# One FFN block instead of two taken plainly before the products by seven

## The chip, the cores and the metric

The kernel runs on one core of a Trainium2 chip. The metric is the device time of one execution in microseconds (us); shown is the median of three runs. A trace of one profiled execution gives start, duration and waits of each instruction on the engines: PE (TensorE, matmuls) with its weight loads (PEld), DVE (VectorE), ACT (ScalarE), POOL (GpSimd) and SP (SyncE, which issues DMAs).

## What is computed

The reference is one layer of a decoder for 1024 prompt positions and 64 sample positions, width 1024: a token mixer (a short convolution and two kinds of attention) with an output projection, then a dense SwiGLU FFN, each behind a modulated RMSNorm. The change touches the FFN alone, and of it the gate and up projections:

```python
def swiglu(h, w_gate_up, w_down):
    gate, up = jnp.split(h @ w_gate_up, 2, axis=-1)
    return (jax.nn.silu(gate) * up) @ w_down

    x = x + gate1 * (mix @ w_out)
    x = x + gate2 * swiglu(rmsnorm(x, g_ffn) * (1 + scale2) + shift2, w_gate_up, w_down)
```

The FFN's inner width is 2816, in the kernel 22 blocks of 128.

## The kernel before

Activations lie transposed: channels on the partitions (eight parts of 128), positions along the row. The 1088 positions are taken in three groups (GRP) of 366, 366 and 356; the third holds the 64 sample positions. Every product in float32 is made of three fast matmuls (mm3, L200, lines 206 to 208): weight and activation are each split into a high and a low part, and high by high, high by low and low by high are summed in PSUM. So each 128 x 512 piece of weights is loaded by SP (load, L97, tile wraw, five buffers), its high part copied by ACT (L92) and its low part subtracted by DVE (L93) into a tile wsp (four buffers). PSUM has three banks with the tag g (ps_g), two each with s and t, and one with o.

The FFN's part of the program runs as follows.

1. While the sample attention streams its caches, the output projection, the second norm and FFN blocks 0 to 3 are done for groups 0 and 1 alone.
2. In the pool "mid", the third group catches up: w_out (L928 ff.), sums of squares and root (second_rstd, rstd, L794), and the normalised, modulated and split activations h2[2] (second_norm, L820; lines 828 to 837 on DVE, ACT and POOL, part by part, in tiles tmp). Behind it in the program, NPRE blocks from block 20 on (FE = 20) make their gate and up products for groups 0 and 1 in the plain way (gate_up, L839), into rows u_ff.
3. In the pool "ffn", blocks 0 to 3 make gate and up for the third group. Between them sums_step (L964, lines 956 to 974) builds the sums of activations that the products by seven need, one of four steps behind each block: 12 DVE operations and 4 ACT copies (L961) a step, in four buffers tw. Then follows the down product of blocks 0 to 3 for the third group: eight output tiles of 12 matmuls, each added to the residual row by add_gated (L773, and for the sample columns L777, which writes ts, and L778).
4. The pairs (20, 21), (4, 5), ... (18, 19) follow. A block that was taken plainly needs the third group only, and a split of its u_ff (L861, L862). Every other block goes through gate_up_2x2 (L977): groups 0 and 1 are seen as a 2 x 2 block matrix with the input halves, and gate and up of both come out of seven products of 4 x 3 matmuls with 366 columns instead of eight; the third group is multiplied plainly beside them (4 x 12 matmuls). POOL makes four combinations of the weights for it (L981 to L984), DVE adds the products up (L1003 to L1023). After each pair its down product for all three groups follows.

The order of instructions on each engine is fixed when the program is built: it is written as above, and a scheduler moves instructions of independent work past each other by its own estimate of times. Each engine then goes through its list in order.

```python
        second_norm(2, second_rstd(2))
        first = [row("u_ff") for _ in range(NPRE)]
        for f, u in enumerate(first):
            gate_up(FE + f, u, None, (0, 1))
...
                if FE <= f < FE + NPRE:
                    u = first[f - FE]
                    split_hid(u, hh, 0, GRP[2][0])
                    gate_up(f, u, hh, (2,))
                else:
                    gate_up_2x2(f, hh)
```

Of the kernel before, what the change touches and what calls it, by code (L numbers as in the profile page):

```python
# [49 lines left out]
FPOOL = ((2, 3, 4), (1, 2, 3, 4, 5), (2, 4, 7))  # L50

MODN = (2, 1, 1, 0, 1, 0, 1, 1, 2, 1, 2, 0)
NPRE = 2

PACE = (1, 1, 1, 1, 0)

# [9 lines left out]
def _build(nc, tc, d, cst, rows, actp, stream, psum):  # L66
# [14 lines left out]
    def row(name):  # L81
        return rows.tile([128, T], F32, tag="row", bufs=ROWS, name=name)
# [734 lines left out]
    def second_rstd(g):  # L817
        return rstd(GRP[g], NADD, acc_tile(g))

    def second_norm(g, r):  # L820
        c0, n = GRP[g]
        m = min(n, SEQ - c0)
        h2[g] = act_tile()
        for k in range(KC):
            t = tmp()
            hi, lo = h2[g][:, 0, k, :n], h2[g][:, 1, k, :n]
            shift = MOD[:, 24 + k, 0:1]
            V.scalar_tensor_tensor(t[:, :m], x1[k][:, c0:c0 + m], MOD[:, 32 + k, 0:1], r[:, :m],
                                   op0=OP.mult, op1=OP.mult)
            S.activation(hi[:, :m], t[:, :m], AF.Identity, bias=shift)  # L830
            V.scalar_tensor_tensor(lo[:, :m], t[:, :m], shift, hi[:, :m].bitcast(F32), op0=OP.add, op1=OP.subtract)
            if g == 2:
                V.tensor_tensor(t[:, m:n], x1[k][:, c0 + m:c0 + n], r[:, m:n], op=OP.mult)
                V.tensor_tensor(bi(t[:, m:n]), bi(t[:, m:n]), modb(32 + k), op=OP.mult)
                V.tensor_tensor(bi(t[:, m:n]), bi(t[:, m:n]), modb(24 + k), op=OP.add)
                S.activation(hi[:, m:n], t[:, m:n], AF.Copy)
                G.tensor_tensor(lo[:, m:n], t[:, m:n], hi[:, m:n].bitcast(F32), op=OP.subtract)
# [87 lines left out]
    with tc.tile_pool(name="mid", bufs=1) as mid:  # L925
# [5 lines left out]
# [3 lines that stand above are left out]
# [3 lines left out]
    with tc.tile_pool(name="ffn", bufs=1, reuse_waits="tile") as ff:  # L937
# [4 lines left out]
        def hid_tile():  # L942
            return ff.tile([128, 2, T], F32R, tag="hid", bufs=2, name="hid")
# [104 lines left out]
        for f0, nf in FF_GROUPS[1:]:  # L1048
            hid = []
            for f in range(f0, f0 + nf):  # L1050
                hh = hid_tile()
                if FE <= f < FE + NPRE:
                    u = first[f - FE]
# [173 lines left out]
```

## Time and profile before

| | us |
|---|---|
| median of 3 runs | 1385.34 |
| lowest, highest | 1382.9, 1385.4 |
| the profiled execution | 1385.72 |
| its span in the trace | 1383.8 |
| mean granted TensorE clock | 0.989 of full speed |

The profiled execution's own time is its span and about 2 us around it. In the page, the first part gives the busy time of each engine; the chain follows the work that ended last back from the end. A row of a timeline is start, duration, engine, line, operation, and in brackets how long the engine had been idle before it and what it waited for. Matmuls overlap: each row shows some 0.33 us, but they start about 0.165 us apart.

### The profile page before, as it was taken

How to read it: one execution, taken by the hardware profiler on the slowest of the kernel's cores; microseconds unless marked ns; L12 is line 12 of the kernel's file. 1: busy time of each engine (PE TensorE's matmuls, PEld its weight loads, DVE VectorE, ACT ScalarE, POOL GpSimd, SP SyncE). 2: the span in 40 equal slices, each digit the busy share in tenths (PEclk: the TensorE clock that was granted, in tenths of full speed). 3: DMA queues.
4: the chain of work that ended last, by engine and by line, in shares of the span. 5: the costliest groups of instructions: out<-in, count | busy, mean ns of one | idle time of the engine just before them, and what ended most of it. 6: DMA issues, size and time to landing. Idle time of an engine off the chain costs nothing.

```text
span 1383.8 us, 23859 instructions
## 1 busy us (share of the span) xinstructions
PE 1340.4 (97%) x9097; PEld 1279.6 (92%) x9097; DVE 851.8 (62%) x2016; ACT 597.0 (43%) x1228; POOL 200.0 (14%) x283
## 2 busy tenths in 40 slices
PE   7999999999999998999999999999999999999994
PEld 5889999988898897889999999999999999999994
DVE  4557768356676336334679766666666666665657
ACT  5487875467765325223355323232323232323243
POOL 2042320201101000000010111111111111111114
PEclk9999999999999999999999999999999999999997
DMA  9342431354415778676544412141414242323103
GB/s 360 117 156 99 139 108 32 117 166 133 146 24 205 269 263 305 209 252 230 155 130 130 123 61 92 48 166 60 154 62 153 76 138 88 133 88 127 45 30 130
DMA packets 77190, 190.90 MB, mean 138 GB/s; under 512 B 14051, under 2 KB 23811, under 8 KB 76291
## 3 DMA queue, kind: packets, MB, share of 16 engines
q1 hardware_dynamic: 73376, 135.67, 29.9%
q10 hardware_dynamic: 3536, 53.65, 10.9%
q8 instruction: 72, 1.18, 0.3%
q14 instruction: 46, 0.35, 0.1%
q0 software_dynamic: 160, 0.04, 0.0%
HBM read 181.32 MB, written 59.33 MB: 174 GB/s over the span
## 4 chain that ended last, share of the span: by engine, by line
PE 87%; DVE 4%; DMA 4%; ACT 3%; issue 2%; POOL 1%; SPq 0%; POOLq 0%; ACTq 0%; DVEq 0%
PE ps_g L206 19%; PE ps_g L207 19%; PE ps_g L208 19%; PE ps_s L207 3%; PE ps_s L206 3%; PE ps_s L208 3%; PE ps_t L206 2%; PE ps_t L207 2%; PE ps_t L208 2%; PE ps_o L584 2%; PE ps_t L575 2%; PE ps_o L703 1%; PE ps_s L531 1%; DMA wraw<-in_w_in 1%; PE ps_s L669 1%
## 5 line engine op out<-in xcount | busy, mean ns | idle before, releaser
L206 PE MATMUL ps_g<-act,wsp 128*128 128x366 f32 (+1 forms) x1192 | 396.7, 334 | 4.3 <-DVE u_ff L846 2.0
L207 PE MATMUL ps_g<-act,wsp 128*128 128x366 f32 (+1 forms) x1192 | 395.3, 332 | 0.0
L208 PE MATMUL ps_g<-act,wsp 128*128 128x366 f32 (+1 forms) x1192 | 392.5, 331 | 0.0
L92 ACT ACTIVATE wsp<-wraw 128x512 fp32r<-128x512 f32 x232 | 145.7, 631 | 286.6 <-PE ps_g L208 185.3
L93 DVE TENSOR_TENSOR wsp<-wraw,wsp 128x512 fp32r<-128x512 f32 x232 | 166.3, 718 | 150.3 <-ACT wsp L92 144.6
L206 PEld LDWEIGHTS ps_g<-act,wsp 128*128 128x128 f32 x1192 | 225.2, 189 | 13.1 <-issue 4.1
L207 PEld LDWEIGHTS ps_g<-act,wsp 128*128 128x128 f32 x1192 | 225.6, 189 | 3.6 <-issue 2.5
L208 PEld LDWEIGHTS ps_g<-act,wsp 128*128 128x128 f32 x1192 | 225.1, 189 | 2.1 <-issue 1.2
L206 PE MATMUL ps_g<-hid,wsp 128*128 128x366 f32 (+3 forms) x464 | 152.6, 331 | 4.2 <-DVE ts L777 3.3
L207 PE MATMUL ps_g<-hid,wsp 128*128 128x366 f32 (+3 forms) x464 | 152.3, 328 | 1.8 <-DVE hid L862 1.7
L208 PE MATMUL ps_g<-hid,wsp 128*128 128x366 f32 (+3 forms) x464 | 152.6, 329 | 0.0
L206 PEld LDWEIGHTS ps_g<-hid,wsp 128*128 128x128 f32 x464 | 87.6, 189 | 6.9 <-issue 3.3
L92 ACT ACTIVATE wsp<-tw 128x512 fp32r<-128x512 f32 x64 | 40.5, 633 | 122.3 <-PE ps_g L208 58.9
L207 PEld LDWEIGHTS ps_g<-hid,wsp 128*128 128x128 f32 x464 | 87.9, 189 | 2.6 <-DVE hid L862 2.4
L207 PE MATMUL ps_s<-act,wsp 128*128 128x366 f32 x272 | 90.2, 332 | 0.0
L206 PE MATMUL ps_s<-act,wsp 128*128 128x366 f32 x272 | 90.1, 331 | 0.0
L208 PE MATMUL ps_s<-act,wsp 128*128 128x366 f32 x272 | 90.0, 331 | 0.0
L208 PEld LDWEIGHTS ps_g<-hid,wsp 128*128 128x128 f32 x464 | 87.8, 189 | 0.0
L773 DVE SCALAR_TENSOR_TENSOR p_q<-ps_g,MOD,p_q 128x366 f32<-128x366 f32 (+3 forms) x99 | 55.5, 571 | 50.4 <-PE ps_g L208 50.3
L773 DVE SCALAR_TENSOR_TENSOR p_qc<-ps_g,MOD,p_qc 128x366 f32<-128x366 f32 (+3 forms) x99 | 56.6, 572 | 35.0 <-PE ps_g L208 33.1
L981 POOL TENSOR_TENSOR tw<-wraw 128x512 f32<-128x512 f32 x16 | 21.9, 1367 | 346.4 <-DMA wraw<-in_w_gu 267.9
L545 ACT ACTIVATE Sb<-Sb,st 128x257 f32<-128x257 f32 (+5 forms) x96 | 60.6, 632 | 20.4 <-DVE st L537 19.7
(337 smaller groups left out, 2319.3 us busy)
## 6 DMA issues: line engine op xcount, KB each, us to landing
wraw<-in_w_gu SPq DMA_DIRECT2D x112, 256.0 KB, 2.8
wraw<-in_wmod SPq DMA_DIRECT2D x64, 256.0 KB, 3.7
raw<-in_bk SPq DMA_DIRECT2D x30, 512.0 KB, 6.2
raw<-in_bv SPq DMA_DIRECT2D x30, 512.0 KB, 7.4
wraw<-in_w_in SPq DMA_DIRECT2D x36, 256.0 KB, 4.2
wraw<-in_w_d SPq DMA_DIRECT2D x36, 256.0 KB, 2.6
mraw<-in_wmod SPq DMA_DIRECT2D x32, 256.0 KB, 5.5
wraw<-in_w_out SPq DMA_DIRECT2D x32, 256.0 KB, 3.2
```

What stands on the lines that cost most here:

```text
L92: S.activation(sp[:, 0, :], raw, AF.Copy)
L93: (V if not state["sub"] or state["n"] % state["sub"] else G).tensor_tensor(sp[:, 1, :], raw, sp[:, 0, :].bitcast(F32), op=OP.subtract)
L206: PE.matmul(ps[:, :n], lhsT=w_hi, rhs=a(0, ak), start=first and j == 0, stop=False, **kw)
L207: PE.matmul(ps[:, :n], lhsT=w_hi, rhs=a(1, ak), start=False, stop=False, **kw)
L208: PE.matmul(ps[:, :n], lhsT=w_lo, rhs=a(0, ak), start=False, stop=last and j == m - 1, **kw)
L531: PE.matmul(ps[:, :sn], lhsT=QH[:, qsl], rhs=KS[hd][:, kk], start=True, stop=False)
L545: S.activation(Sb[:, :ne], Sb[:, :ne], AF.Exp, scale=-1.0, bias=m, accum_out=st[:, 3:4])
L575: PE.transpose(pt[:, col:col + 128], Sb[:, (kb - k0) * 128:(kb - k0 + 1) * 128], ident)
L584: PE.matmul(po[:, q0:q0 + w], lhsT=Vt[:, kb, hd].rearrange("p a b -> p (a b)"), rhs=PT[:, hl, c0:c0 + w], start=fresh, stop=ch is chunks[- ...
L669: PE.matmul(ps[32 * j:32 * j + 32, :n], lhsT=Q[:, 2 * j + par, :], rhs=keys[par][:, j, :n], start=(par == 0), stop=(par == 1))
L773: ins = V.scalar_tensor_tensor(x1[m][:, c0:c0 + k], ps[:, :k], MOD[:, gate + m, 0:1], x1[m][:, c0:c0 + k], op0=OP.mult, op1=OP.add)
L981: G.tensor_tensor(t1, b12, b11, op=OP.subtract)
```

## The change

```diff
-NPRE = 2
+NPRE = 1
```

Block 21's gate and up products for groups 0 and 1 are no longer made in step 2, and its third group no longer by the plain form in step 4. Block 21 goes through gate_up_2x2 as blocks 4 to 19 do. Block 20 stays as it is.

On PE, the first place is the end of block 20's plain up product (ps_g with wsp_8106 before and wsp_8105 after; act_6253 and act_6278 are groups 0 and 1, act_7935 is the third group). Before:

```order
L208 MATMUL ps_g_8074<-act_6278,wsp_8106 128x366
L206 MATMUL ps_g_8135<-act_6253,wsp_8139 128x366
L207 MATMUL ps_g_8135<-act_6253,wsp_8139 128x366
L208 MATMUL ps_g_8135<-act_6253,wsp_8139 128x366
L206 MATMUL ps_g_8135<-act_6253,wsp_8139 128x366
```

Now:

```order
L208 MATMUL ps_g_8073<-act_6278,wsp_8105 128x366
L206 MATMUL ps_g_8148<-act_7935,wsp_8151 128x356
L207 MATMUL ps_g_8148<-act_7935,wsp_8151 128x356
L208 MATMUL ps_g_8148<-act_7935,wsp_8151 128x356
L206 MATMUL ps_g_8148<-act_7935,wsp_8151 128x356
```

The 96 matmuls of block 21 on groups 0 and 1 are gone from here; block 0's gate for the third group, which reads the newly normalised tile, comes directly behind block 20.

On DVE, the second place is behind the third group's normalisation, where the sums begin (tw, sa and act_6278 are written by sums_step, wsp are weight splits, u_ff_8009 is block 21's row, u_8147 block 0's row for the third group). Before:

```order
L967 TENSOR_TENSOR tw_8350<-tw_8348,tw_8350 128x366
L93 TENSOR_TENSOR wsp_8313<-wraw_8311,wsp_8313 128x512
L969 TENSOR_TENSOR tw_8348<-tw_8352,tw_8348 128x366
L962 TENSOR_TENSOR sa1_8268<-tw_8350,sa1_8268 128x366
L846 TENSOR_TENSOR u_ff_8009<-u_ff_8009,ps_g_8198 128x366
L971 TENSOR_TENSOR tw_8352<-tw_8350,tw_8352 128x366
L962 TENSOR_TENSOR act_6278<-tw_8348,act_6278 128x366
```

Now:

```order
L967 TENSOR_TENSOR tw_8224<-tw_8222,tw_8224 128x366
L969 TENSOR_TENSOR tw_8222<-tw_8226,tw_8222 128x366
L93 TENSOR_TENSOR wsp_8282<-wraw_8280,wsp_8282 128x512
L962 TENSOR_TENSOR sa1_8142<-tw_8224,sa1_8142 128x366
L971 TENSOR_TENSOR tw_8226<-tw_8224,tw_8226 128x366
L962 TENSOR_TENSOR act_6278<-tw_8222,act_6278 128x366
L846 TENSOR_TENSOR u_8147<-u_8147,ps_g_8184 128x356
L93 TENSOR_TENSOR wsp_8299<-wraw_8297,wsp_8299 128x512
```

The sums stand at the same place behind the normalisation; the splits between them now belong to blocks 0 and 1 of the third group, and block 21's multiplication is gone.

On DVE, the third place is in the third group's down product of blocks 0 to 3 (L773 and L777 read its output tiles: before 8697 is the third, 8719 the fourth; now 8571 the third, 8593 the fourth). Before:

```order
L773 SCALAR_TENSOR_TENSOR p_q0_2107<-ps_g_8697,MOD_106,p_q0_2107 128x292
L93 TENSOR_TENSOR wsp_8744<-wraw_8742,wsp_8744 128x512
L778 TENSOR_TENSOR cv_2828<-cv_2828,ts_8672 128x64
L93 TENSOR_TENSOR wsp_8766<-wraw_8764,wsp_8766 128x512
L778 TENSOR_TENSOR cv_4877<-cv_4877,ts_8694 128x64
L93 TENSOR_TENSOR wsp_8788<-wraw_8786,wsp_8788 128x512
L777 TENSOR_TENSOR ts_8716<-ps_g_8697,MOD_106 128x64
```

Now:

```order
L773 SCALAR_TENSOR_TENSOR p_q0_2107<-ps_g_8571,MOD_106,p_q0_2107 128x292
L93 TENSOR_TENSOR wsp_8618<-wraw_8616,wsp_8618 128x512
L969 TENSOR_TENSOR tw_8507<-tw_8511,tw_8507 128x366
L93 TENSOR_TENSOR wsp_8640<-wraw_8638,wsp_8640 128x512
L962 TENSOR_TENSOR sa1_8142<-tw_8509,sa1_8142 128x366
L778 TENSOR_TENSOR cv_2828<-cv_2828,ts_8546 128x64
L93 TENSOR_TENSOR wsp_8662<-wraw_8660,wsp_8662 128x512
L778 TENSOR_TENSOR cv_4877<-cv_4877,ts_8568 128x64
L971 TENSOR_TENSOR tw_8511<-tw_8509,tw_8511 128x366
L773 SCALAR_TENSOR_TENSOR p_q1_3224<-ps_g_8593,MOD_106,p_q1_3224 128x292
L962 TENSOR_TENSOR act_6278<-tw_8507,act_6278 128x366
L93 TENSOR_TENSOR wsp_8684<-wraw_8682,wsp_8684 128x512
```

The next row now is L777 of tile 8571. Before, all sums were done ahead of this place; now the last step's stand between the down product's evacuations, four of them ahead of the third tile's L777, and so does the fourth tile's L773.

## The prediction

> **What bounds the kernel now.** I read the page first: which engine is full, and what the chain that ended last is made of.
>
> ```profile
> PE 1340.4 (97%) x9097; PEld 1279.6 (92%) x9097; DVE 851.8 (62%) x2016; ACT 597.0 (43%) x1228; POOL 200.0 (14%) x283
> PE 87%; DVE 4%; DMA 4%; ACT 3%; issue 2%; POOL 1%; SPq 0%; POOLq 0%; ACTq 0%; DVEq 0%
> ```
>
> PE is busy for 97% of the span and holds 87% of the chain, so a matmul that goes away should be worth its own time, unless another engine comes to be late. DVE's 62% is an average; what counts is its share in the stage that the change shortens. That stage runs from the first plain gate and up product of block 20 to the end of block 21's third group. The second view is a table of busy times by stretch; the third is the chain of waits cut to 690 to 800 us.
>
> ```profile
> 691.70:725.30 33.60, 33.60 (x207) 33.60 (x206) 23.43 (x70) 17.71 (x36) 3.61 (x8) 1.00 0.41 133
> 725.30:757.00 31.70, 31.70 (x195) 31.70 (x194) 30.30 (x62) 18.20 (x37) 0.00 (x0) 1.00 0.43 126
> 757.00:772.70 15.70, 15.51 (x97) 15.25 (x96) 11.57 (x32) 6.08 (x10) 0.00 (x0) 1.00 0.45 135
> 772.70:788.40 15.70, 15.70 (x98) 15.70 (x97) 9.16 (x15) 6.92 (x13) 1.29 (x1) 1.00 0.43 132
> by line: PE ps_g L206 32.6%; PE ps_g L207 32.0%; PE ps_g L208 31.8%; PE ps_s L207 0.6%; PE ps_s L811 0.6%; PE ps_s L206 0.6%; PE ps_s L208 0.6%; PE ps_t L807 0.5%; DVE cv L773 0.5%; issue 0.1%; DVE ts L777 0.1%
> ```
>
> The columns after the stretch's length are busy us of PE, PEld, DVE, ACT and POOL. PE never stops before 757 us, but in 725.3 to 757 DVE is busy 30.30 of 31.70 us. There are two nearly full engines side by side. The change takes 16 us of PE work out from in front of that stretch, and hardly any DVE work.
>
> **The matmuls.** PE's rows give the stage borders (start us, duration); the last row is the page's group for POOL's weight combinations.
>
> ```profile
> 691.71 0.33 PE L206 MATMUL ps_g<-act,wsp 128*128 128x366 f32 x1
> 704.17 0.41 PE L207 MATMUL ps_g<-act,wsp 128*128 128x366 f32 x1
> 725.27 0.32 PE L206 MATMUL ps_g<-act,wsp 128*128 128x356 f32 x1
> 772.66 0.33 PE L206 MATMUL ps_g<-act,wsp 128*128 128x356 f32 x1
> 788.36 0.33 PE L206 MATMUL ps_g<-hid,wsp 128*128 128x366 f32 x1
> L981 POOL TENSOR_TENSOR tw<-wraw 128x512 f32<-128x512 f32 x16 | 21.9, 1367 | 346.4 <-DMA wraw<-in_w_gu 267.9
> ```
>
> Blocks 20 and 21, groups 0 and 1: 192 matmuls and the norm's few small ones, from 691.71 to 725.27. The last 125 of them start at 704.17 (counted in the order, behind the small ones at L811) and take 21.1 us, 0.169 each; block 21's 96 are 16.2 us, so block 20 ends near 709.0. The next 288 matmuls (192 of gate and up, 96 of the down product, all third group) take 47.4 us, 0.1645 each; 96 more, to 788.36, finish the two plain blocks.
>
> Block 21 was 96 + 48 = 144 matmuls. By seven products it is 7 x 12 = 84 plus the same 48: 132. Removed: 12 x 0.169 = **2.0 us** of PE. Splits stay at eight for the block and loads go from eight to four; POOL gets four operations of 1.37 us (the L981 row) and DVE seven operations where two multiplications stood before. These lie in the stretch after 757 us, where DVE is busy 9.16 to 11.57 of 15.70 us, so I cost them at nothing; without that cover POOL's four would cost 5.5 us.
>
> **The third group's normalisation.** In the order, PE's next work after block 20 now needs it; before, block 21 stood in between. DVE, ACT and POOL make it, part by part (eight parts of 128 channels); POOL's operation ends each.
>
> ```profile
> 704.46 0.52 DVE L828 SCALAR_TENSOR_TENSOR tmp<-cv,MOD,ps_s 128x292 f32<-128x292 f32 x1 [1.50 <-PE ps_s L811]
> 710.26 0.32 POOL L837 TENSOR_TENSOR act<-tmp,act 128x64 fp32r<-128x64 f32 x1 [1.21 <-ACT act L836]
> 713.83 1.03 POOL L837 TENSOR_TENSOR act<-tmp,act 128x64 fp32r<-128x64 f32 x2 [3.25 <-ACT act L836]
> 718.97 0.66 POOL L837 TENSOR_TENSOR act<-tmp,act 128x64 fp32r<-128x64 f32 x1 [0.34 <-ACT act L836]
> 704.40:719.40 15.00, 13.80 (x47) 1.00 0.43 141
> 719.40:759.30 39.90, 37.56 (x77) 1.00 0.41 119
> ```
>
> The last two rows are DVE alone: 13.80 of 15.00 us busy in the norm, so it will not come sooner. DVE's order there is the same as before but for one split. From 709.0 PE has parts 0 to 2: 18 matmuls, 3.0 us, to 712.0. Part 3 ends near 714.3: PE idles 2.3 us. After that parts arrive about as fast as PE uses them, with the next block's gate in between, and the last is there at 719.6. This wait alone costs **2.3 us**; the eight parts' covering work was block 21.
>
> **DVE after the normalisation.** This is the larger term. Behind the norm DVE's order has the sums for the products (48 operations), mixed with the splits that PE needs at once. The ends and the paces come from these rows:
>
> ```profile
> 716.75 0.94 DVE L831 SCALAR_TENSOR_TENSOR act<-tmp,MOD,act 128x292 fp32r<-128x292 f32 x2
> 718.78 0.69 DVE L93 TENSOR_TENSOR wsp<-wraw,wsp 128x512 fp32r<-128x512 f32 x1 [0.95 <-ACT wsp L92]
> 727.59 0.69 DVE L93 TENSOR_TENSOR wsp<-wraw,wsp 128x512 fp32r<-128x512 f32 x1
> 728.19 0.54 DVE L962 TENSOR_TENSOR sa<-tw,sa 128x366 fp32r<-128x366 f32 x1
> 728.64 0.54 DVE L967 TENSOR_TENSOR tw<-tw 128x366 f32<-128x366 f32 x1
> 762.10 0.52 DVE L773 SCALAR_TENSOR_TENSOR cv<-ps_g,MOD,cv 128x292 f32<-128x292 f32 x1 [2.82 <-PE ps_g L208]
> 762.54 0.22 DVE L777 TENSOR_TENSOR ts<-ps_g,MOD 128x64 f32<-128x64 f32 x1
> 762.67 0.52 DVE L773 SCALAR_TENSOR_TENSOR cv<-ps_g,MOD,cv 128x292 f32<-128x292 f32 x1
> 762.90 0.41 PE L206 MATMUL ps_g<-hid,wsp 128*128 128x356 f32 x1 [0.19 <-DVE ts L777]
> ```
>
> Start to start, a split takes 0.60 us, a sum 0.45, an evacuation 0.44, the short copy ts 0.13. The down product has three PSUM banks: its fourth tile waits for ts of the first (the 762.90 row), its sixth for ts of the third. In the new order 80 DVE operations run from the first sum up to that ts: 18 splits, 45 sums, 12 of 0.44 and 5 of 0.13, 10.8 + 20.3 + 5.3 + 0.7 = 37.0 us. The same sum over before's 76 operations up to 759.3 gives 36.8, and the window measured 37.56 busy; scaled, 37.7. The first sum can start when the norm's last operation is done, 717.7, and one split more stands ahead: 718.3. I add 0.6 of idle at the first split, whose buffer PE frees only with the norm's last part. So the sixth tile starts at 718.3 + 37.7 + 0.6 = 756.6, and three tiles of 12 matmuls, 5.9 us, end the stage at 762.5. From 709.0 that is 53.5 us where before needed 47.4: **+6.1 us**. The 2.3 us of the norm lies inside it, since DVE, not PE, sets the end. Bounds: with DVE's idle between 0 and the 2.3 us that it had before, and a start between 718.2 and 719.4, the end is 761.8 to 765.3, so +5.4 to +8.9; below, if DVE's work doesn't hold PE at all, only 2.3.
>
> **The new pair border.** Block 21 as products ends with a split that the down product waits for. Before, this pair had no such wait at 788.36; the later pairs show what it costs:
>
> ```profile
> 859.65 0.44 PE L207 MATMUL ps_g<-hid,wsp 128*128 128x366 f32 x1 [1.75 <-DVE hid L862]
> 929.86 0.44 PE L206 MATMUL ps_g<-hid,wsp 128*128 128x366 f32 x1 [0.15 <-DVE cv L773]
> 998.29 0.44 PE L206 MATMUL ps_g<-hid,wsp 128*128 128x366 f32 x1 [0.24 <-DVE cv L773]
> 857.48 1.72 POOL L983 TENSOR_TENSOR tw<-wraw 128x512 f32<-128x512 f32 x1
> 858.00 1.60 DVE L862 TENSOR_TENSOR hid<-u,hid 128x366 fp32r<-128x366 f32 x1
> ```
>
> I take **+0.2 us**, as most do. The bound above is about 2.0 (the 1.75 and 0.15 to 0.24 behind it): at 858.00 DVE's split took 1.60 us beside POOL, against 0.54 for the like operation at 728.19. If that collision moves away from the pair at 859, the change gains 2.0 instead.
>
> **The clock.** PE's rows after a wait of like size, and the granted clock (behind the count):
>
> ```profile
> 577.79 0.44 PE L206 MATMUL ps_g<-act,wsp 128*128 128x366 f32 x1 [2.00 <-DVE u_ff L846]
> 579.00:582.50 3.50, 3.50 (x14) 0.51 0.93 336
> 582.50:585.00 2.50, 2.50 (x18) 1.00 0.80 231
> 860.00:865.00 5.00, 4.76 (x26) 1.00 0.16 61
> ```
>
> After 2.00 us of idle the clock was 0.51 for 3.5 us, 1.7 us lost; after the 1.75 us at 859.65 it stayed at 1.00. My two waits (2.3 at the norm, about 2 at the down product's sixth tile) stand near the first. A fall at the norm is hidden, since DVE sets the end; one at the sixth tile is not. I take nothing, with 1.7 us as the other end. [...]
>
> **Sum.** -2.0 + 6.1 + 0.2 = **+4.3 us** on the profiled execution's 1385.72 us (span 1383.8): 1390.0. The median of the three runs is 0.4 lower; from it, 1389.6. PE is full to the last group, so nothing behind the stage takes this back.
>
> **Rivals.** (1) *Only the norm's wait costs*: DVE keeps ahead because PE, once late by 2.3 us, asks later. -2.0 + 2.3 + 0.2 = +0.5: 1385.8. For it: DVE is not late for any split in before. Against: PE would reach the sixth tile at 709.0 + 252 x 0.1645 + 2.3 = 752.8, 34.5 us after DVE's first sum (718.3), and DVE needs 37.7. (2) *More is lost*: the clock falls at the sixth tile and the new border costs 2.0 instead of 0.2: 4.3 + 1.7 + 1.8 = +7.8: 1393.1. For it: the rows at 577.79 and 858.00. Against: both happened once each. (3) *Faster*: the saved matmuls are kept and the collision at 859 disperses, -2.0 - 2.0 + 0.2 = -3.8: 1381.5. It decides at the sixth tile: unhindered, PE wants it at 709.0 + 252 x 0.1645 = 750.5, so the 37.7 us of DVE work must begin by 712.8, or PE must not need them; the norm holds DVE to 717.7. That block 21 stays plain is excluded by the order.
>
> **How the numbers follow.** Forecast 0.52, only the norm 0.22, more lost 0.20, faster 0.06. Some 0.2% (2.8 us) is what a measurement of this kernel can tell from no change, so slower is 0.72, same 0.22, faster 0.06. The range takes in (1) and (2), with 0.3 us below and 1.4 above, the latter for DVE's upper bound: 1385.5 to 1394.5.
>
> **What would show it.** After: a PE wait of about 2 us near 712 us for the third group's act tile; DVE without gaps from there to about 756; a PE wait on ts at the down product's sixth tile; block 21's products with no wait on POOL's tiles. If PE is full between 709 and 762, the sum is wrong at its largest term; if DVE is late by far more, it was its pace.

## The result and the profile after

| kernel | median, us (runs) | ratio to the kernel before | profiled execution: span, us |
|---|---|---|---|
| before | 1384.70 (11) | 1 | 1383.8 |
| after the change | 1388.90 (11) | 1.0035 [1.002, 1.005] | 1387.1 |

One of the eleven executions of before, 1863.61 us, was in a slow state and is not in the ratio. The change costs 0.35%, 2.8 to 6.9 us by the interval. The sum forecast 4.3 us, 1389.6 as a median; the two medians are 4.2 us apart, the two profiled spans 3.3. The page of after, its first part and the shares of the chain that ended last:

```profile
PE 1335.5 (96%) x9085; PEld 1274.5 (92%) x9085; DVE 858.1 (62%) x2022; ACT 597.5 (43%) x1230; POOL 206.0 (15%) x287
PE 84%; DVE 7%; DMA 4%; issue 2%; ACT 2%; POOL 1%; SPq 0%; POOLq 0%; ACTq 0%; DVEq 0%
```

The twelve matmuls are gone (9097 before, 9085 now), yet the span grew, and DVE's share of the chain went from 4% to 7%. PE's timeline of after gives the stage borders and the waits between them (start, duration, operation, and in brackets the idle time and its releaser):

```profile
691.04 0.33 PE L206 MATMUL ps_g<-act,wsp 128*128 128x366 f32 x1
708.49 0.32 PE L206 MATMUL ps_g<-act,wsp 128*128 128x356 f32 x1
713.13 0.59 PE L206 MATMUL ps_g<-act,wsp 128*128 128x356 f32 x2 [1.55 <-ACT act L836]
749.22 0.40 PE L206 MATMUL ps_g<-hid,wsp 128*128 128x356 f32 x1 [1.09 <-DVE ts L777]
755.25 0.41 PE L206 MATMUL ps_g<-hid,wsp 128*128 128x356 f32 x1 [1.92 <-DVE ts L777]
762.71 0.33 PE L206 MATMUL ps_g<-act,wsp 128*128 128x356 f32 x1
770.55 0.33 PE L206 MATMUL ps_s<-act,wsp 128*128 128x366 f32 x1
792.51 0.33 PE L206 MATMUL ps_g<-hid,wsp 128*128 128x366 f32 x1
795.19 0.44 PE L207 MATMUL ps_g<-hid,wsp 128*128 128x366 f32 x1 [0.84 <-DVE hid L862]
828.58 0.32 PE L206 MATMUL ps_g<-act,wsp 128*128 128x356 f32 x1
```

Block 20 ends at 708.49. The third group's 288 matmuls take from there to 762.71, 54.22 us where before needed 47.39 (725.27 to 772.66). Block 20's own third group and block 21's products follow without a wait to 792.51, and the pair's down product takes to 828.58: 36.07 us, where before's first pair took 33.83 (788.36 to 822.19). All of this is in places that the prediction named. In the same stretches (columns as in the prediction: busy us of PE, PEld, DVE, ACT, POOL, then granted clock, DMA share, GB/s):

```profile
691.00:708.50 17.50, 17.50 (x111) 17.50 (x110) 9.10 (x29) 9.73 (x16) 0.68 (x2) 1.00 0.39 131
708.50:740.50 32.00, 30.32 (x184) 29.74 (x184) 31.75 (x78) 19.31 (x43) 2.82 (x6) 1.00 0.36 111
740.50:762.70 22.20, 19.19 (x107) 18.66 (x107) 21.45 (x52) 9.65 (x18) 1.60 (x1) 0.92 0.40 119
770.50:792.50 22.00, 22.00 (x134) 22.00 (x133) 10.81 (x18) 8.27 (x15) 2.21 (x2) 1.00 0.32 109
```

From 708.5 to 762.7 DVE is busy 53.20 of 54.20 us, and PE 49.51: DVE has taken PE's place as the full engine there. DVE's own rows put the ends close to the forecast, the first sum at 717.81 (718.3 expected) and the ts for which the sixth down tile waits at 754.89:

```profile
717.81 1.08 DVE L956 TENSOR_TENSOR tw<-act 128x366 f32<-128x366 f32 x2
754.89 0.22 DVE L777 TENSOR_TENSOR ts<-ps_g,MOD 128x64 f32<-128x64 f32 x1
717.81:754.89 37.08, 37.05 (x81) 1.00 0.42 128
```

The last row is DVE alone between these two: busy for 37.05 of 37.08 us.

One row above is unlike the rest: a clock of 0.92 in 740.5 to 762.7. Cut finer, it is this:

```profile
752.49:756.49 4.00, 2.08 (x12) 1.82 (x11) 4.00 (x11) 1.37 (x3) 0.00 (x0) 0.95 0.61 192
756.49:760.49 4.00, 4.00 (x18) 4.00 (x18) 3.37 (x10) 0.80 (x2) 1.03 (x1) 0.62 0.29 104
```

After the 1.92 us wait the clock fell: PE shows 18 matmuls in 4 us, where it has 27 in this profile's 4 us from 716.49 and 26 in those from 759.49, both at a clock of 1.00. That is the fall that the prediction named with 1.7 us as an end of its range and took as nothing.

At the new border, DVE's two splits of hid stand beside POOL's weight combinations for the next pair (t3 is POOL's third of four):

```profile
793.01 1.73 POOL L983 TENSOR_TENSOR tw<-wraw 128x512 f32<-128x512 f32 x1
793.52 1.61 DVE L862 TENSOR_TENSOR hid<-u,hid 128x366 fp32r<-128x366 f32 x1
796.60 1.44 DVE L862 TENSOR_TENSOR hid<-u,hid 128x356 fp32r<-128x356 f32 x1
```

A DVE operation of this size took 0.54 us where POOL was quiet (the row at 728.19 in the prediction), here three times that. PE's wait of 0.84 us at 795.19 is the longest piece of the 2.24 us; the rest lies in shorter gaps behind it.

### The profile page after: what moved, and what is told of

Read it like the earlier page. It is cut to its first block, busy times and chain, and to the rows that moved or that the text cites. A ratio compares the mean times of both kernels' runs of the same rounds, so it can differ in the third digit from the quotient of the medians.

```text
span 1387.1 us, 23844 instructions
## 1 busy us (share of the span) xinstructions
PE 1335.5 (96%) x9085; PEld 1274.5 (92%) x9085; DVE 858.1 (62%) x2022; ACT 597.5 (43%) x1230; POOL 206.0 (15%) x287
## 4 chain that ended last, share of the span: by engine, by line
PE 84%; DVE 7%; DMA 4%; issue 2%; ACT 2%; POOL 1%; SPq 0%; POOLq 0%; ACTq 0%; DVEq 0%
PE ps_g L206 18%; PE ps_g L207 18%; PE ps_g L208 17%; PE ps_s L207 4%; PE ps_s L206 4%; PE ps_s L208 3%; PE ps_t L206 3%; PE ps_t L207 3%; PE ps_t L208 3%; PE ps_o L584 2%; DMA wraw<-in_w_gu 2%; PE ps_t L575 2%; DVE wsp L93 2%; PE ps_s L531 1%; PE ps_s L532 1%
## 5 line engine op out<-in xcount | busy, mean ns | idle before, releaser
L206 PE MATMUL ps_g<-act,wsp 128*128 128x366 f32 (+1 forms) x1160 | 385.3, 334 | 8.7 <-DVE u_ff L846 4.9
L207 PE MATMUL ps_g<-act,wsp 128*128 128x366 f32 (+1 forms) x1160 | 384.5, 332 | 0.1
L208 PE MATMUL ps_g<-act,wsp 128*128 128x366 f32 (+1 forms) x1160 | 381.4, 331 | 0.0
L93 DVE TENSOR_TENSOR wsp<-wraw,wsp 128x512 fp32r<-128x512 f32 x228 | 162.5, 714 | 153.9 <-ACT wsp L92 147.8
L206 PEld LDWEIGHTS ps_g<-act,wsp 128*128 128x128 f32 x1160 | 218.7, 189 | 17.8 <-DVE u_ff L846 5.5
L207 PEld LDWEIGHTS ps_g<-act,wsp 128*128 128x128 f32 x1160 | 219.3, 189 | 3.8 <-issue 2.3
L208 PEld LDWEIGHTS ps_g<-act,wsp 128*128 128x128 f32 x1160 | 218.5, 189 | 2.1 <-issue 1.2
L207 PE MATMUL ps_s<-act,wsp 128*128 128x366 f32 x288 | 95.5, 332 | 0.0
L206 PE MATMUL ps_s<-act,wsp 128*128 128x366 f32 x288 | 95.5, 331 | 0.0
L208 PE MATMUL ps_s<-act,wsp 128*128 128x366 f32 x288 | 95.2, 331 | 0.0
L773 DVE SCALAR_TENSOR_TENSOR p_q<-ps_g,MOD,p_q 128x366 f32<-128x366 f32 (+3 forms) x99 | 55.4, 570 | 48.9 <-PE ps_g L208 48.8
L773 DVE SCALAR_TENSOR_TENSOR p_qc<-ps_g,MOD,p_qc 128x366 f32<-128x366 f32 (+3 forms) x99 | 56.5, 571 | 35.3 <-PE ps_g L208 33.5
```

The lines of the kernel that those rows point to most:

```text
L93: (V if not state["sub"] or state["n"] % state["sub"] else G).tensor_tensor(sp[:, 1, :], raw, sp[:, 0, :].bitcast(F32), op=OP.subtract)
L206: PE.matmul(ps[:, :n], lhsT=w_hi, rhs=a(0, ak), start=first and j == 0, stop=False, **kw)
L207: PE.matmul(ps[:, :n], lhsT=w_hi, rhs=a(1, ak), start=False, stop=False, **kw)
L208: PE.matmul(ps[:, :n], lhsT=w_lo, rhs=a(0, ak), start=False, stop=last and j == m - 1, **kw)
L773: ins = V.scalar_tensor_tensor(x1[m][:, c0:c0 + k], ps[:, :k], MOD[:, gate + m, 0:1], x1[m][:, c0:c0 + k], op0=OP.mult, op1=OP.add)
```

## The experiments

Two lengths say more than a median that scatters by several us. The **stretch** runs from the plain block's first matmul (691.04 in after, 691.71 in before) to the first pair's down product (792.51, 788.36). A border is a pair's down product, with the first products of the next block mixed in, from its first matmul to the next block's long run of third-group matmuls (792.51 to 828.58); its **excess** is what it takes over the 33.83 us that it needs undisturbed. There are eight. Both are differences of PE start times, read in each kernel's profile in the same way. In the table the first four rows are the two profiles above and one more of each kernel. From e1 on, each ratio is to the kernel before as run again beside that experiment (medians of 1383.1 to 1384.2 us there), so it is not the quotient of two medians of the table.

| kernel | stretch | excess, 1st border | 2nd | 3rd to 8th | median | ratio |
|---|---|---|---|---|---|---|
| before | 96.65 | 0 | 3.14 | 2.18 | 1384.70 | 1 |
| before, again | 96.64 | 0 | 2.79 | 1.68 | 1383.02, one run | |
| after | 101.47 | 2.24 | 2.20 | 0.78 | 1388.90 | 1.0035 |
| after, again | 99.89 | 2.28 | 1.28 | 0.79 | 1387.56, one run | |
| e1, banks | 99.21 | 2.50 | 2.21 | 2.17 | 1387.15 | 1.0030 |
| e2, two steps of sums held | 106.42 | 2.72 | 0.28 | 0.90 | 1393.25 | 1.0079 |
| e3, the other block plain | 100.75 | 0.89 | 1.28 | 2.64 | 1387.01 | 1.0031 |
| e4, no block plain | 108.25 | 2.38 | 2.38 | 2.40 | 1401.62 | 1.0134 |
| e7, one step of sums held | 98.39 | 2.30 | 1.28 | 2.07 | 1385.52 | 1.0024 |
| e8, lighter sums | 96.82 | 2.39 | 1.27 | 2.35 | 1385.26 | 1.0017 |
| e11, POOL held | 99.90 | 0 | 0 | 0 | 1381.94 | 0.9994 |
| e12, all three | 101.73 | 0 | 0 | 0 | 1386.63 | 1.0021 |
| e13, before with POOL held | 96.64 | 0 | 0 | 0 | 1379.67 | 0.9973 |
| e15, sums and POOL held | 98.36 | 0 | 0 | 0 | 1380.91 | 0.9991 |

(e4 has no plain block; its stretch starts where the w_out matmuls of the third group end, at 693.07, 2.73 us ahead of the row at 695.80 below.) The theory to test: *DVE's work behind the norm sets the end of the stage*. Rivals: the PSUM banks set it; the norm's wait alone does; the loss is at the borders.

**More PSUM banks for the third group's down product (e1).** Its tiles go through seven banks instead of three:

```diff
-                ps = ps_tile("g")
+                ps = ps_tile("gst"[m % 3])
```

> The changed kernel, but the third group's down product of blocks 0 to 3 takes its PSUM banks from the tags g, s and t in turn (seven banks) instead of g alone (three). Theory: DVE, kept full by the sums behind the normalisation, holds PE through the evacuations of the three banks; with seven banks the two waits on ts (1.1 and 1.9 us in the changed kernel) and the half clock behind them (1.7 us) go, and only a split or two is late. The stage of 288 third-group matmuls takes 50 to 51 us instead of 54.2, the kernel 3 to 4.5 us less than the changed one: 1384.5 to 1386. Rival (the loss is at the normalisation's own wait near 712 us and at the new pair border): no change, 54 us for the stage, 1388 to 1389.

Measured: 1387.15 us, ratio 1.0030 [1.001, 1.005], above what was expected. No wait on ts is left, but PE isn't full either. The one wait over 0.2 us in the down product, and the table by stretch around it (here the scheduler also mixes the matmuls of neighbouring tiles):

```profile
749.34 0.43 PE L208 MATMUL ps_s<-hid,wsp 128*128 128x356 f32 x1 [0.31 <-DVE wsp L93]
744.00:748.00 4.00, 4.00 (x25) 3.46 (x23) 2.98 (x8) 2.32 (x5) 0.00 (x0) 1.00 0.02 4
748.00:752.00 4.00, 3.69 (x20) 3.17 (x21) 4.00 (x10) 1.81 (x4) 0.00 (x0) 1.00 0.31 78
```

In 748 to 752 PE did 20 matmuls at full clock, where the 4 us before have 25, now for want of split weights (wsp, L93), which DVE makes as well and for which it is busy all 4.00 us. So the wait moved from one DVE product to another, though not in full: the stretch, 99.21 us, is 0.7 below that of after again (99.89), and 0.8 above that of e7 below, whose clock fell at the norm's wait as it did here. That the bank was only the place of the wait, and DVE's lateness its cause, this run makes likely; e7 and e8 show it.

**Two of four steps of sums held back (e2).** Steps 2 and 3 are put behind DVE's evacuation of the third and the sixth down tile:

```diff
-                sums_step(f)
+                if f < 2:
+                    sums_step(f)
...
-                add_gated(m, GRP[2], ps, 40)
+                ins = add_gated(m, GRP[2], ps, 40)
+                if m in (2, 5):
+                    with tc.issue_after(ins.ins):
+                        sums_step(2 + m // 3)
```

> The changed kernel, but the third and fourth step of the sums (24 of the 48 DVE operations) are ordered behind the third and sixth tile of the third group's down product, where DVE has room. Nothing else moves. Theory (the sums make DVE late for PE): DVE reaches the third tile's ts some 9 us earlier, both waits on ts and the half clock go, the stage takes 49 to 50 us instead of 54.2, and the kernel 3.5 to 5 us less than the changed one, 1384 to 1385.5; block 21's first products may wait up to 1 us for their sums. Rival (the wait for the normalisation, not DVE's work behind it, makes the loss): unchanged, 1388 to 1389.

Measured: 1393.25 us, ratio 1.0079 [1.005, 1.0109]: the opposite. The stage itself is better, with no wait on ts over 0.19 us and 51.14 us (705.40 to 756.54) where 49 to 50 were expected; the clock had fallen at the norm's wait. Then PE stops in block 21's products:

```profile
740.00:744.00 4.00, 4.00 (x27) 4.00 (x25) 1.91 (x4) 1.06 (x2) 0.00 (x0) 1.00 0.65 173
768.95 1.44 POOL L981 TENSOR_TENSOR tw<-wraw 128x512 f32<-128x512 f32 x1 [53.35 <-DVE tw L971]
772.62 0.67 PE L206 MATMUL ps_t<-sa,wsp 128*128 128x366 f32 x1 [4.09 <-ACT wsp L92]
774.48 0.67 PE L208 MATMUL ps_t<-sa,wsp 128*128 128x366 f32 x1 [0.88 <-DVE wsp L93]
```

DVE was held too long: half idle in 740 to 744, and then the sums ended so late that POOL, which shares their four buffers tw, could begin block 21's weights only at 768.95 (behind DVE's tw at L971). PE waited 4.09 us, the clock was at 0.55 to 0.59 from 772 to 780, and more was lost than won. Work moved out of one stage has to fit in front of the next.

**Block 21 plain instead of block 20 (e3).** Same amount of work; now the pair's second block is the plain one.

```diff
-            gate_up(FE + f, u, None, (0, 1))
+            gate_up(FE + 2 - NPRE + f, u, None, (0, 1))
...
-                if FE <= f < FE + NPRE:
-                    u = first[f - FE]
+                if FE + 2 - NPRE <= f < FE + 2:
+                    u = first[f - FE - 2 + NPRE]
```

> The changed kernel, but of the pair 20 and 21 it is block 21 that is taken plainly ahead of the normalisation and block 20 that goes by products, so the pair ends with a plain third group as it did before the change. Theory: what the new pair border costs (2.2 us between the last product of block 21 and the next block's plain part) comes from the last split of a block by products, held up beside POOL; with the plain block last it goes, 1.5 to 2.2 us less than the changed kernel: 1386.7 to 1387.4. The stage of the third group keeps its 54 us. Rival (the border costs the same whichever block is last, or block 20's products wait for the sums instead): within 0.5 us of the changed kernel, or slower.

Measured: 1387.01 us, ratio 1.0031 [1.0012, 1.0049]: the time lies in the theory's range, but the ratio is that of after within 0.0004, so it doesn't tell the theory from its rival. The excess of the first border fell from 2.24 to 0.89 us, and its wait on hid is gone; the largest wait left in it is this row:

```profile
793.50 0.44 PE L206 MATMUL ps_g<-hid,wsp 128*128 128x366 f32 x1 [0.42 <-DVE cv L773]
```

So the new border's wait on hid comes from a block of products standing right before the down product, as predicted of its kind. Its size was not: most later borders of before had shown 0 to 0.8. Nor was anything gained in all: the eight borders sum to 4.8 us, against 4.4 to 5.2 in after.

**No block plain (e4).** NPRE = 0.

> No block is taken plainly ahead (0 instead of 1), so PE has no cover at all. Theory: 2 us of matmuls are saved again; the normalisation starts some 6 us earlier and DVE's work behind it ends some 6 us earlier, at about 757 us instead of 762.7, since DVE and not PE sets the end; both blocks by products take 44 us. So the pair's down product starts near 801 us instead of 792.5: 6 to 11 us more than the changed kernel, 1395 to 1400. Rival (each block of cover costs what the first did): 4 us more, 1393. Rival (PE's own cover counts in full, 16 us a block): 14 us more, 1403.

Measured: 1401.62 us, ratio 1.0134 [1.0105, 1.0163]: 12.7 us more than after's median, above the theory's 6 to 11 and nearer to the rival's 14. The part that the theory is about came as expected: the first border begins at 801.32 (801 expected), 8.8 us later than after's, 6.8 of it in the stretch. The rest of the two profiles' difference lies behind that place, 1.9 us in the borders and 1.6 behind the last of them. Now the norm stands bare, with the clock at 0.50 from 696.3 to 706.6, and ts is late on top of it:

```profile
695.80 0.38 PE L807 MATMUL ps_t<-ones,acc 128*128 128x1 f32 x2 [2.73 <-DVE acc L804]
703.50 0.96 PE L206 MATMUL ps_g<-act,wsp 128*128 128x356 f32 x2 [3.56 <-ACT act L836]
751.86 0.40 PE L206 MATMUL ps_g<-hid,wsp 128*128 128x356 f32 x1 [1.46 <-DVE ts L777]
```

From two plain blocks to one the stretch grows by 3.2 to 4.8 us, from one to none by 6.8 to 8.4: the cover is worth more, the less there is of it.

**Only the last step of sums held (e7), and sums with less DVE work (e8).** e7 holds step 3 alone, behind the third down tile; e8 lets ACT write the low parts of the sums as plain copies, so that only its times are of use.

```diff
-                sums_step(f)
+                if f < 3:
+                    sums_step(f)
...
-                add_gated(m, GRP[2], ps, 40)
+                ins = add_gated(m, GRP[2], ps, 40)
+                if m == 2:
+                    with tc.issue_after(ins.ins):
+                        sums_step(3)
```

```diff
-            V.tensor_tensor(lo, t, hi.bitcast(F32), op=OP.subtract)
+            S.activation(lo, t, AF.Copy)
```

> One block plain; only the last of the four steps of sums is held, until DVE has evacuated the third tile of the third group's down product. Theory (DVE's order inside the stage delays PE: the sums stand ahead of what PE waits for; in the run that held two steps PE ran the down product without a wait on ts, with DVE idle for about 6 us before it): no PE wait on ts, no fall of the clock at the sixth tile, the stage 50 to 51.5 us instead of 54.2, and the held 5.4 us of DVE work still done by about 759, before the products of block 21 ask for it. Time 3 to 4 below after: 1384.5 to 1386. Rival (a held step is paid in the products as before, however small): a PE wait on wsp or sa of 3 us or more between 755 and 780, time as after or worse, 1388 to 1392.

> One block plain; the 16 low parts of the sums are written by ACT as copies instead of by DVE as differences (so the products of the blocks have a wrong low part: the kernel leaves those differences out). Theory (the amount of DVE work in the stage sets its end): 16 x 0.45 = 7.2 us less on DVE, more than the 4.2 by which DVE is late at the sixth tile (754.9 against 750.5), so no PE wait on ts, the stage 49.5 to 51 us, time 3.5 to 4.5 below after. Rival (the waits come from PSUM and the order, not from the amount): the waits of 1.1 and 1.9 us on ts stay, time within 1 us of after.

Measured: e7 1385.52 us, ratio 1.0024 [1.0007, 1.0042]; e8 1385.26 us, 1.0017 [0.9998, 1.0036]. The times alone would not settle it; the traces do. In each, the only wait on ts left in the stage (e7, then e8) is the small one that before has too:

```profile
745.05 0.40 PE L206 MATMUL ps_g<-hid,wsp 128*128 128x356 f32 x1 [0.19 <-DVE ts L777]
```

```profile
742.40 0.41 PE L206 MATMUL ps_g<-hid,wsp 128*128 128x356 f32 x1 [0.19 <-DVE ts L777]
736.20:752.20 16.00, 15.81 (x99) 15.55 (x98) 12.20 (x34) 8.43 (x16) 0.06 (x1) 1.00 0.50 149
```

e8's stage takes 49.58 us (702.58 to 752.16), e7's 51.12 (703.68 to 754.80; its clock fell at the norm's wait, see the last section), against 54.22 and 52.64 in the two profiles of after. In e8's down product DVE is busy 12.20 of 16.00 us, where in after it had no slack. Both the amount and the order of DVE's work decide: the theory holds. And e8's stretch, 96.82, is within 0.2 us of before's: all that is left there is the norm's wait, 49.58 - 47.39 = 2.2 us, which eats the 2.0 us of matmuls saved.

**The same two kernels again (e9, e10).** One more profile of each, unchanged.

> The changed kernel once more, for one profile. If the excess of the pair borders over 33.83 us (2.24, 2.20, 0, 0.77, 0.01 in the first profile) belongs to the kernel, it comes again within 0.3 at each border; if it is a matter of the phase of one execution, the borders differ by 1 us or more while the third group's stage stays at 54.2 within 0.5.

> The kernel before once more, for one profile. If the excess of the borders (0, 3.14, 0.63, 0.72, 0.83) belongs to the kernel, it comes again within 0.3 at each; if it is the phase of one execution, the second border differs by 1 us or more while the third group's stage stays at 47.4 within 0.3.

Neither expectation came out whole. The first border's excess repeats (2.28 against 2.24; 0 against 0), the second moves by 0.9 us in after and 0.35 in before, most of the later ones come and go by 0.6 to 0.9 each. The stage of before repeats at 47.38, but that of after was 52.64, 1.58 below the first, outside the 0.5 expected. PE's waits on ts are the same, 1.04 and 1.92 us. The clock isn't: after the second wait the clock of this execution stays at 1.00:

```profile
751.87:755.87 4.00, 2.08 (x14) 1.82 (x13) 4.00 (x11) 1.38 (x3) 0.00 (x0) 1.00 0.66 176
755.87:759.87 4.00, 4.00 (x27) 4.00 (x27) 3.94 (x14) 1.55 (x4) 1.13 (x1) 1.00 0.46 141
```

27 matmuls where the first profile shows 18. So the fall is a matter of the execution, not of the kernel.

**POOL held at the borders (e11, and e13 on the kernel before).** POOL's four combinations for a pair's first block wait until DVE has split the previous pair's last hid; one column of that hid is copied by POOL ahead of them, to carry the wait. PE first needs one of the results some 16 us after the border's start (788.66 to 804.53 in e11).

```diff
-        def gate_up_2x2(f, hh):
+        def gate_up_2x2(f, hh, ahead_of=None):
...
+            held_by = ExitStack()
+            if ahead_of is not None:
+                jk = sp_.tile([128, 1], F32, tag="jk", bufs=2, name="jk")
+                one = G.tensor_copy(jk, ahead_of[:, 1, c2:c2 + 1].bitcast(F32))
+                held_by = tc.issue_after(one.ins)
+            with held_by:
+                G.tensor_tensor(t1, b12, b11, op=OP.subtract)
...
-                    gate_up_2x2(f, hh)
+                    gate_up_2x2(f, hh, prev if f == f0 else None)
```

> The changed kernel, and in it POOL's four differences for the first block of each later pair wait (behind a one-column copy of the previous pair's last hid) until DVE has split that hid. Theory (the excess of a border is DVE's splits and evacuations slowed beside POOL): DVE's split of 366 columns takes 0.54 us there instead of 1.4 to 1.6, the excess falls from 2.2 to about 0.4 at the first border and from 1.3 to 2.2 to about 0.4 at the second, the sum of the excess over the borders from 4.4 to 5.2 to 1 to 2: 1385 to 1386.5, the third group's stage unchanged (52.6 or 54.2 us). Rival (the wait is set by PE's chain through the last products, or the raw weights held longer delay the loads): the excess stays within 0.5, or a new wait on tw or wsp of over 1 us appears in the products, and the time is that of the changed kernel or 1 to 3 above.

> The kernel before (two blocks plain) with POOL's differences held at the borders alone. Theory: its first border has no excess in any case, the second falls from about 3 us to about 0.4, the others from 0 to 0.8 to 0 to 0.4: 2.5 to 4 us less than before, 1380 to 1382, and it stays 2 to 4 below the changed kernel with the same hold, which is then the cost of the change without its borders. Rival (the borders aren't POOL's doing): same time as before, within 1 us.

Measured: e11 1381.94 us, ratio 0.9994 [0.9978, 1.001]; e13 1379.67 us, ratio 0.9973 [0.9952, 0.9995]. Both are a little better than expected: all eight borders take 33.83 or 33.84 us in both, within 0.01 of the undisturbed length, where up to 0.4 us of excess had been expected to stay at each. The first border of e11, the same two splits as above and POOL behind them:

```profile
788.44 0.54 DVE L862 TENSOR_TENSOR hid<-u,hid 128x366 fp32r<-128x366 f32 x1
790.88 0.52 DVE L862 TENSOR_TENSOR hid<-u,hid 128x356 fp32r<-128x356 f32 x1
791.64 1.29 POOL L987 TENSOR_TENSOR tw<-wraw 128x512 f32<-128x512 f32 x1
```

1.61 and 1.44 us became 0.54 and 0.52. Later DVE operations beside POOL are still slowed (a split at 796.11 takes 1.23 us beside POOL's operation of 1.29 at 795.50, where others in e11 take 0.69), but PE no longer waits for them. e13 gains 0.27% on the kernel before and is the fastest of all here. Its profiled execution was the longest of its twelve (1375.99 to 1387.38), having lost 5 us and more ahead of the plain blocks, so its median is taken for the time and its profile for the stretch and the borders alone. With the borders quiet in both, the change alone is left: 99.90 - 96.64 = 3.3 us in the stretch. The medians are 2.3 us apart, but the twelve times of one kernel overlap with those of the other (e11 1381.07 to 1387.55), so they alone wouldn't show it.

**All three repairs (e12).** e3, e7 and e11 together; the diffs are those above.

> One block plain, and it is the second of the pair; the last step of sums held; POOL's differences held at the borders: all three repairs. Theory (they add up): the stretch from the plain block to the first border about 97 to 98.5 us (before 96.6), the excess of the borders about 1 us in all where before has 4.5 to 5.3, so 1380 to 1382.5, ratio to before 0.997 to 0.999. Rival (the repairs disturb each other, as the swap changes DVE's order in the stage): a PE wait on ts comes back in the stage, 1384 to 1387.

Measured: 1386.63 us, ratio 1.0021 [0.9998, 1.0043]: the rival's price, but not its wait. The borders are quiet, ts isn't late, and still the stretch is 101.73. With block 21 plain, no plain third group stands between the stage and the first products, and the held sums and POOL meet right in front of them: POOL's first combination waits for a late sum, and two of DVE's splits beside it take 1.72 us each instead of 0.69.

```profile
759.51 1.47 POOL L987 TENSOR_TENSOR tw<-wraw 128x512 f32<-128x512 f32 x1 [42.79 <-DVE tw L971]
763.55 3.44 DVE L93 TENSOR_TENSOR wsp<-tw,wsp 128x512 fp32r<-128x512 f32 x2
763.37 0.44 PE L206 MATMUL ps_t<-sa,wsp 128*128 128x366 f32 x1 [1.37 <-ACT wsp L92]
765.36 0.43 PE L208 MATMUL ps_t<-sa,wsp 128*128 128x366 f32 x1 [1.39 <-DVE wsp L93]
```

**Two repairs, without the swap (e15).** e7 and e11 together.

> One block plain, the last step of sums held, POOL's differences held at the borders; block 20 stays the plain one. Theory (what is left of the change is the wait of the norm, about 2.2 us, against the 2.0 us of products saved; a fall of the clock at that wait adds 1.5): no wait on ts or wsp over 0.2 us, the stretch from the plain block to the first border 96.8 us without and 98.4 with the fall, all borders 33.83; about 3 us (2 to 4.5) less than the changed kernel, 1380 to 1382, level with the kernel before under the same hold (1379.67) or up to 2 us above it. Rival (as in the run with all three repairs, the held step and POOL's differences get in each other's way in the first products): PE waits on wsp of 1 us and more between 755 and 780, the stretch over 99.5 us, time 1383 or more.

Measured: 1380.91 us, ratio 0.9991 [0.9976, 1.0005]; stretch 98.36, all borders quiet, the one wait on ts 0.19 us. That is the theory's number for an execution in which the clock falls at the norm's wait, and it did fall:

```profile
712.00:716.00 4.00, 3.88 (x17) 3.59 (x17) 3.78 (x14) 2.56 (x7) 1.56 (x4) 0.70 0.09 7
```

Without the swap, then, the two holds don't disturb each other. Even so repaired, the change gains nothing on the kernel before with the same hold (1379.67).

## Why the prediction was right

The terms, against the two pairs of profiles:

| term | predicted | first pair | second pair |
|---|---|---|---|
| twelve matmuls fewer | -2.0 | -2.01 | -2.01 |
| the third group's stage, without the clock | +6.1 | +5.25 | +5.26 |
| fall of the clock in it | 0 | +1.58 | 0 |
| the pair borders, all eight | +0.2 | -0.10 | -0.12 |
| sum | +4.3 | +4.7 | +3.1 |

The stage of the first pair is 54.22 - 47.39 = 6.83; its clock is the 1.58 us by which the two profiles of after differ. The spans of the two pairs are 3.3 and 4.9 us apart. What the terms leave over, -1.4 and +1.8 us, lies ahead of the stretch (-0.7 and +1.1) and behind the last border (-0.7 and +0.7), where the change alters nothing: it is scatter from execution to execution, as large as some of the terms.

*The matmuls* came out to the hundredth: 33.56 + 15.70 us of them before (691.71 to 725.27, 772.66 to 788.36), 17.45 + 29.80 after.

*DVE as the bound of the stage* was the right mechanism, and e7 and e8 show it: the loss goes when DVE has less to do, or when the sums step aside. The size was 0.9 us too large. The sums began 9.3 us behind block 20's end, as forecast (708.49 to 717.81). From there to the sixth tile I had 38.3 us and it was 37.4: the 0.6 us of idle that I added was not there, and the counted 37.0 us (DVE was busy 37.05) were nearer than their scaled 37.7. The lateness showed in two waits, 1.09 us at the fourth tile and 1.92 at the sixth, where I named the sixth alone; since DVE sets the end, the sum is the same.

*The norm's wait* lies inside the stage as forecast. The wait itself is 1.55 us and not 2.3, since PE was let go by ACT's high part of the next piece (L836) and not, as I had it, by POOL's operation that ends it; there are smaller gaps behind it; e8's stage, where nothing else is late, is 2.2 us longer than before's, against the 2.3 forecast. Rival 1 (only this wait costs) is thus what a kernel with lighter sums would show, not this one.

*The clock* is the term that I priced at nothing and that costs 1.6 us in one of two executions. The two rows I had, a fall after 2.00 us and none after 1.75, couldn't settle the choice between its ends; in these profiles the length of the wait alone doesn't decide it (below). That waits of 2 us and more cost no clock, no row that I had showed: it was my estimate. The runs showed 1.58 us lost behind the 1.92 us wait in after and nothing in after again.

*The border* was right in the net and wrong in its place. The new border costs 2.2 us, the upper bound, and not 0.2; the step that failed was to take the price from most later borders instead of from the one at 859 us. Reading single waits made it too small besides: the rows with 0.15, 0.24 and 1.75 us stand in borders whose excess is 0.63, 0.72 and 3.14. But the next border gave back 0.9 to 1.5 us, which is the part of rival 3 about the collision moving, and the later ones, which come and go between executions, 0.9 to 1.4. The sum over all borders is 4.4 to 5.3 us in both kernels, before and after alike: a cost that was there all along.

That the net came within 1.2 us of the forecast is then partly luck: a stage 0.9 too dear against a clock that costs 0 or 1.6, and a new border 2 us too cheap against others that gave as much back.

## What to carry to other kernels

An engine at 62% over the span can be full in the one stage that a change shortens, so count its operations between two events there, and ask where the wait goes when one of its products is relieved: with more PSUM banks PE waited for wsp in place of ts. Work held back must still fit in front of its consumer, with the buffers it shares; one held step helped, two made the stretch 5 us longer. And where a short operation stands alone between two stages of PE, keep POOL off DVE's back at that moment: by the ratios, one ordering constraint gave 0.41% in the changed kernel and 0.27% in the one before, where the change cost 0.35%.

## What the runs showed of the hardware

The clock fell after waits shorter than the 2.00 us of the prediction's row, and not every time. The norm's wait of 1.55 or 1.56 us is there in ten profiles with one plain block. In six (e1, e2, e3, e7, e12, e15) the clock then stood at 0.50 for 3.4 us; in four (after, after again, e8, e11) it stayed at 1.00. The 4 us in which the wait ends, in after:

```profile
712.49:716.49 4.00, 3.23 (x18) 2.94 (x19) 3.78 (x15) 2.62 (x8) 1.21 (x3) 1.00 0.11 41
```

Where nothing else held the stage's end, the fall cost some 1.5 us: e7's stage against e8's, 51.12 - 49.58. The longer wait on ts of 1.9 us had it in one of three profiles (after, but neither after again nor e11).

In three profiles the starts of the falls, read from the granted clock in each trace, lie whole multiples (steps) of 3.413 us apart (in before, 102.40 us for 30 of them). In e15 they begin at 577.03, 713.57, 1355.27 and 1365.51 us, which is 40, 188 and 3 steps, and the first two last one step each (PE alone: busy, clock, DMA share, GB/s):

```profile
577.03:580.45 3.42, 3.42 (x13) 0.50 0.91 323
713.57:716.98 3.41, 3.41 (x13) 0.50 0.33 80
```

In before they begin at 428.91, 531.31, 579.09, 1360.74 and 1370.98 us, 30, 14, 229 and 3 steps apart, in after at 366.96, 756.08 and 1373.89 us, 114 and 181 steps apart. Counted in steps from the start of the span they leave a rest of 0.18 us in e15, 2.24 in before and 1.73 in after, so the starting point was another in each. Of the five waits of 1.55 to 2.0 us that this document names in these three profiles, the three behind which the clock fell (577.79 in before, 755.25 in after, the norm's in e15) began 0.1, 0.7 and 0.0 us into a step, the two others (859.65 in before, 713.13 in after) 2.3 and 3.3 us into one. So what looks like chance went, in these five, with the place of the wait among the steps. It wasn't the whole rule: in before a wait of 2.79 us, ending at 532.48, began 1.8 us into a step and the clock fell at 531.31, and in after one of 3.03 us, ending at 596.82, began 1.6 us into one and no fall came.

DVE beside POOL: in after the 366-column split took 1.61 us beside POOL's operation of 1.73 (793.01), the 356-column one 1.44 beside one of 1.28 (796.37). In e11, with POOL's operations behind them, the two took 0.54 and 0.52 us, and POOL's like ones 1.28 to 1.29. The 1.61 and the 1.73 us are each nearly the sum of the two shorter times (0.54 + 1.29 = 1.83).
